# A residual block in fp32r terms on one core: sixteen gate and up chunk pairs of the second feed-forward as 2 by 2 block products with seven products, and all down weight sums made in the first feed-forward

## The chip, the cores and the metric

One core of one Trainium2 chip runs the whole program in one launch. The metric is device time in microseconds (us) of that core. Three runs of the kernel before gave 1135.78, 1136.21 and 1136.25 us; the median is 1136.21.

## The reference

One decoder layer on x of 512 tokens by 1024 features, in fp32. Cut to what matters here:

```
f = swiglu(rms_norm(h, ffn1_pre_g), ffn1_w_gu, ffn1_w_down)
h = h + 0.5 * rms_norm(f, ffn1_post_g)
m = hybrid_mixer(rms_norm(h, mix_pre_g), ...)
h = h + rms_norm(m, mix_post_g)
f = swiglu(rms_norm(h, ffn2_pre_g), ffn2_w_gu, ffn2_w_down)
h = h + 0.5 * rms_norm(f, ffn2_post_g)

def swiglu(x, w_gu, w_down):
    g, u = jnp.split(x @ w_gu, 2, axis=-1)
    return (silu(g) * u) @ w_down
```

`w_gu` is 1024 by 2 x 2816 and `w_down` 2816 by 1024. 2816 is 22 chunks of 128.

## The kernel before

**Terms.** Each fp32 operand is split into a high and a low part in the matmul's fp32r form, and one product is three matmuls into the same PSUM bank (`mm3`, L147-L150): high by high, high by low, low by high. A weight chunk of 128 x 1024 comes from DRAM into a `wraw` buffer (SP issues the load, L109; six buffers). ACT copies it to the high part (L118), and DVE subtracts that from the raw chunk for the low part (L119). `wsplit` does both, two chunks ahead of the one that `wget` hands out (AHEAD), and the load is asked for six chunks ahead (RAHEAD).

**Stages.** f1 is the first feed-forward: `gate_up` and then `strassen_out`, the down projection. The mixer follows (projections, recurrence, attention, two output projections). f2 is the second feed-forward, with the same two functions.

**gate_up** goes through 22 chunk pairs. Pair j is one gate chunk and one up chunk of 128 of the 2816 columns. Each chunk is `feat_chunk` (L245): 8 slices of 128 features, each a product of 128 x 128 weights by 512 tokens, so 24 matmuls into one bank of 128 x 512, and 48 for the pair. `tail` (L313) then makes silu(gate) times up: in f2 a tanh on ACT (L319) and two DVE operations (L323, L324), in f1 one more DVE operation ahead (L321, the row's norm factor). The pairs of the first half (c of h = 0) and of the second (h = 1) are kept apart, for the down projection. In f2 the first two pairs are `first_four` (L254): four banks, and each chunk in two passes of 256 tokens, so that PE can begin when half of the tokens are normalised.

**Down projection.** `strassen_out` takes the down weights as 2 by 2 blocks (two halves of the 2816 features by two halves of the output columns), and the hidden values as 2 by 2 blocks too (feature halves by token halves), with seven products rather than eight. That needs sums of weight blocks and of hidden blocks. `weight_sums` (L270) makes the weight sums during gate_up of the same stage: for each of 11 chunks it loads two raw chunks (L275), makes four adds of 128 x 512 on DVE (L280), and stores the four sums to DRAM (L282), from where the down projection loads them as weights. Its steps are spaced in ticks, one tick for each weight chunk that PE has been given: three ticks for a chunk of sums. `sum_pairs` (L288) makes the sums of hidden blocks for two pairs at a time (L294, L295, L297).

**Order.** The scheduler places instructions on in-order engine queues by the order of the program and by buffers coming free. Buffers around the change: 19 of 8 KB for split weights, sums and operands (`b8`), 6 raw weight buffers, 4 of 4 KB (`t4`), 11 of 2 KB (`t2`), 8 PSUM banks.

## Time and profile before

| | |
|---|---|
| median of three runs | 1136.21 us |
| the profiled execution | 1135.31 us |
| its span, first to last instruction | 1133.2 us |
| PE busy | 1125.1 us of the span, 5318 matmuls |
| DVE busy | 741.1 us |
| ACT busy | 491.9 us |
| moved by DMA | 192.68 MB, mean 170 GB/s |
| granted TensorE clock | 0.999 |
| f1 gate_up | from 4.7 to 295 us |
| f2 gate_up | from 779.8 to 1022 us |

The profile comes from one profiled execution. PE, DVE, ACT, POOL and SP are the engines; PEld is the loading of weights into PE, which overlaps with matmuls. In a row of a list of groups stand the line, the engine, the operation, out<-in by names, the shape and the count, then busy time and mean duration. In a timeline row stand the start and the duration in us, then engine, line and operation; `xN` means N instructions in a run. Square brackets give the idle time ahead of it and what ended that. A matmul's duration covers the pipeline from its start to its last column, so its pace is read from start to start. What lies outside the span is 1135.31 - 1133.2 = 2.1 us.

### The profile page before, as it was taken

The page shows a single profiled execution, that of the slowest core. Times are in us where ns is not written, and L with a number is a line of the kernel's source. Part 1 is how long each engine was busy: PE and PEld are TensorE (multiplying, and loading weights), DVE is VectorE, ACT ScalarE, POOL GpSimd, SP SyncE. Part 2 cuts the span into 40 slices and gives each one's busy share as a digit, 9 for nine tenths or more (in the row PEclk, how much of TensorE's full clock was granted, in tenths as well). Part 3 has the DMA queues.
Part 4 walks back from the last instruction along what each step waited for, and adds up shares of the span by engine and source line. Part 5 has one row for each costly group of instructions (what it writes and reads, how often), then busy time and mean ns, then how long its engine had stood idle before and what let it go on. Part 6 is the DMA issues. An engine that isn't in the chain of part 4 may idle for free.

```text
span 1133.2 us, 14097 instructions
## 1 busy us (share of the span) xinstructions
PE 1125.1 (99%) x5318; PEld 938.0 (83%) x5318; DVE 741.1 (65%) x1122; ACT 491.9 (43%) x767; POOL 25.0 (2%) x47
## 2 busy tenths in 40 slices
PE   9999999999999999999999999999999999999997
PEld 7888888888888887888888888889888888888886
DVE  5674475677787779796776745636553564648784
ACT  6332122255754588453655633414331131236671
POOL 1000000000000000000000000001000000000001
PEclk9999999999999999999999999999999999999999
DMA  9773493546766213334211323533636655616582
GB/s 362 275 288 135 177 333 118 203 152 194 231 248 223 93 64 104 112 98 136 83 57 56 106 81 103 210 134 123 259 129 252 223 206 199 227 60 203 190 281 75
DMA packets 63957, 192.68 MB, mean 170 GB/s; under 512 B 7824, under 2 KB 8592, under 8 KB 61072
## 3 DMA queue, kind: packets, MB, share of 16 engines
q1 hardware_dynamic: 59136, 176.56, 44.2%
q10 hardware_dynamic: 4752, 15.21, 3.8%
q8 instruction: 42, 0.69, 0.2%
q14 instruction: 27, 0.22, 0.1%
HBM read 160.28 MB, written 29.36 MB: 167 GB/s over the span
## 4 chain that ended last, share of the span: by engine, by line
PE 98%; ACT 2%; DVE 0%; issue 0%; POOLq 0%; POOL 0%; DVEq 0%
PE f1g L149 7%; PE f1g L150 7%; PE f1g L148 7%; PE f2g L149 6%; PE f2g L148 6%; PE f2g L150 6%; PE f1x L148 2%; PE f1x L149 2%; PE f2x L148 2%; PE f2x L150 2%; PE f2x L149 2%; PE f1x L150 2%; PE glg L148 1%; PE gag L148 1%; PE gt L150 1%; PE gag L149 1%
## 5 line engine op out<-in xcount | busy, mean ns | idle before, releaser
L119 DVE TENSOR_TENSOR w<-wraw,w 128x1024 fp32r<-128x1024 f32 x238 | 278.7, 1189 | 39.1 <-ACT w L118 38.3
L118 ACT CAST w<-wraw 128x1024 fp32r<-128x1024 f32 x238 | 233.3, 1023 | 105.4 <-PE f1g L150 18.3
L149 PE MATMUL f1g<-u1l,w 128*128 128x512 f32 x336 | 130.8, 389 | 0.0
L148 PE MATMUL f1g<-u1h,w 128*128 128x512 f32 x336 | 130.8, 389 | 0.0
L150 PE MATMUL f1g<-u1h,w 128*128 128x512 f32 x336 | 130.7, 389 | 0.0
L148 PE MATMUL f2g<-b2uh,w 128*128 128x512 f32 x320 | 124.5, 389 | 0.0
L149 PE MATMUL f2g<-b2ul,w 128*128 128x512 f32 x320 | 124.5, 389 | 0.0
L150 PE MATMUL f2g<-b2uh,w 128*128 128x512 f32 x320 | 124.5, 389 | 0.0
L319 ACT ACTIVATE f2s<-f2g 128x512 f32<-128x512 f32 x20 | 12.0, 600 | 145.0 <-PE f2g L150 145.0
L148 PEld LDWEIGHTS f1g<-u1h,w 128*128 128x128 f32 x336 | 63.1, 188 | 13.2
L149 PEld LDWEIGHTS f1g<-u1l,w 128*128 128x128 f32 x336 | 63.1, 188 | 13.2
L150 PEld LDWEIGHTS f1g<-u1h,w 128*128 128x128 f32 x336 | 63.1, 188 | 12.9
L148 PEld LDWEIGHTS f2g<-b2uh,w 128*128 128x128 f32 x320 | 60.1, 188 | 12.5
L150 PEld LDWEIGHTS f2g<-b2uh,w 128*128 128x128 f32 x320 | 60.1, 188 | 12.5
L149 PEld LDWEIGHTS f2g<-b2ul,w 128*128 128x128 f32 x320 | 60.1, 188 | 12.3
L322 ACT ACTIVATE f1s<-f1s 128x512 f32<-128x512 f32 x22 | 13.9, 632 | 128.5 <-DVE f1s L321 128.5
L324 DVE SCALAR_TENSOR_TENSOR f2p<-f2s,f2g 128x512 f32<-128x512 f32 x20 | 13.7, 686 | 58.1 <-PE f2g L150 58.1
L323 DVE SCALAR_TENSOR_TENSOR f2s<-f2s,f2g 128x512 f32<-128x512 f32 x20 | 13.7, 685 | 45.2 <-ACT f2s L319 45.2
L324 DVE SCALAR_TENSOR_TENSOR f1p<-f1s,f1g 128x512 f32<-128x512 f32 x22 | 15.0, 686 | 42.3 <-PE f1g L150 42.1
L321 DVE TENSOR_TENSOR f1s<-f1g,rows 128x512 f32<-128x512 f32 x22 | 15.1, 689 | 32.8 <-PE f1g L150 32.7
L148 PE MATMUL glg<-b1uh,w 128*128 128x512 f32 x64 | 25.8, 403 | 0.0
L148 PE MATMUL glp<-ylh,w 128*128 128x512 f32 x64 | 25.4, 397 | 0.0
(720 smaller groups left out, 2450.4 us busy)
## 6 DMA issues: line engine op xcount, KB each, us to landing
wraw<-in_gu_dram SPq DMA_DIRECT2D x86, 512.0 KB, 5.4
wraw<-t_spill SPq DMA_DIRECT2D x88, 256.0 KB, 3.8
wraw<-in_dn_dram SPq DMA_DIRECT2D x66, 256.0 KB, 5.3
f1tr<-in_dn_dram SPq DMA_DIRECT2D x22, 512.0 KB, 6.4
t_spill<-f1ts SPq DMA_DIRECT2D x11, 1024.0 KB, 7.5
f2tr<-in_dn_dram SPq DMA_DIRECT2D x22, 512.0 KB, 6.4
t_spill<-f2ts SPq DMA_DIRECT2D x11, 1024.0 KB, 7.5
wraw<-in_w_x_dram SPq DMA_DIRECT2D x8, 512.0 KB, 4.5
```

Of the source, the lines that this page charges most:

```text
L118: A.copy(w[:, 0, :end], raws[n][:, :end])
L119: V.tensor_tensor(out=w[:, 1, :end], in0=raws[n][:, :end], in1=w[:, 0, :end].bitcast(F32), op=ALU.subtract)
L148: PE.matmul(o, lhsT=ah, rhs=bh, start=start, stop=False, skip_group_check=more)
L149: PE.matmul(o, lhsT=ah, rhs=bl, start=False, stop=False, skip_group_check=more)
L150: PE.matmul(o, lhsT=al, rhs=bh, start=False, stop=stop, skip_group_check=more)
L319: A.activation(s, bg, AF.Tanh, scale=0.5)
L321: V.tensor_tensor(out=s, in0=bg, in1=rows, op=ALU.mult)
L322: A.activation(s, s, AF.Tanh, scale=0.5)
L323: V.scalar_tensor_tensor(out=s, in0=s, scalar=1.0, in1=bg, op0=ALU.add, op1=ALU.mult)
L324: V.scalar_tensor_tensor(out=ps[h][-1][:, c % 4, :], in0=s, scalar=0.5, in1=bu, op0=ALU.mult, op1=ALU.mult)
```

## The change

**Block products.** Pairs 3 to 18 of f2 (BLOCK_PAIRS) are no longer two chunks of 24 matmuls. The 1024 features are halved, the 512 tokens are halved, and gate and up form the third index: four outputs of 128 x 256, each a sum over two feature halves. The scheme of the down projection gives them with seven products. A product is 4 slices of 128 features, three matmuls each, of 128 x 256: 12 matmuls, 84 for the pair. PE's order within a pair is p1 into bank X, p7 into Y, p6 onto X, p2 into Z, q5 onto X, q4 into Y, q3 onto X (`Blocks.run`). Between them ACT and DVE take partial sums out of the banks: `kv` is p1 in its first half and p7 in its second, `ua` is X after p6 and after q5, `up` and `g` are the up and gate outputs.

**Operands.** The sums of input blocks are made once (`Blocks.operands`, during first_four): two adds of 128 x 2048 on DVE that join high and low again, four sums of 128 x 1024, and four splits of 128 x 1024. Each pair needs four sums of weight blocks of 128 x 512 on DVE (`steps`), and splits of 1024 columns three times and of 512 once (ACT copy, DVE subtract): the gate chunk `g`, the sums `st` 1 and 0, and `d`. The weights of pair j + 1 are made while pair j runs. ACT's and DVE's order in these pairs is written out (`line` chains each instruction behind the one before).

**Weight sums.** Both sets of 11 chunks of down weight sums are made in f1's gate_up, the second set for f2, at 1, 1, 2, 2 ticks a chunk, and none in f2. The next raw chunks are loaded right behind the store.

**Hidden sums.** For the block pairs `sum_pairs` runs once for up to four pairs, behind the last block pair (`later`).

The diff, cut to its core:

```
+BLOCK_PAIRS = range(3, 19)
...
-        while len(wready) < min(upto, len(worder)):
+        while len(wready) < min(upto, len(worder), *stops[:1]):
...
                 if tok is HALVES[1]:
+                    next(extra, None)
                     done(i, bs[i])
...
-    def weight_sums(dn, scr, name, wait):
+    def weight_sums(wait):
         yield wait
-        for c in range(KH):
-            raw = b8(f"{name}tr{c}", [P, 2, 1024])
-            for i in range(2):
-                SP.dma_start(raw[:, i, :], dn[c + i * KH])
-            yield 2
+        todo_ = [(dn, scratch[f], f, c) for f, dn in enumerate((dn1, dn2)) for c in range(KH)]
+        loaded = []
+
+        def load():
+            if len(loaded) < len(todo_):
+                dn, _, f, c = todo_[len(loaded)]
+                raw = b8(f"tr{f}{c}", [P, 2, 1024])
+                for i in range(2):
+                    SP.dma_start(raw[:, i, :], dn[c + i * KH])
+                loaded.append(raw)
+
+        load()
+        yield 2
+        for n, (dn, scr, f, c) in enumerate(todo_):
+            raw = loaded[n]
             b11, b12, b21, b22 = (raw[:, i, hc] for i in range(2) for hc in (slice(0, 512), slice(512, 1024)))
-            ts = b8(f"{name}ts{c}", [P, 4, 512])
+            ts = b8(f"ts{f}{c}", [P, 4, 512])
             for o, a, b in ((0, b11, b12), (1, ts[:, 0], b22), (2, ts[:, 1], b21), (3, b12, b22)):
                 V.tensor_tensor(out=ts[:, o], in0=a, in1=b, op=ALU.add)
-            yield 1
             SP.dma_start(scr[c], ts)
-
-    def gate_up(u, name, dn, scr, rows=None, marks=None):
+            load()
+            yield 1 + n % 4 // 2
...
+        def operands(self, marks):
+            u, name, (A1, A2) = self.u, self.name, self.toks
+            self.ops, self.last["v"] = {}, marks["low", NT - 1]
+            (a, b), xs = self.f, self.xs
+            for i in range(2):
+                self.line("v", V.tensor_tensor, out=self.f[i], in0=u[0][i].bitcast(F32), in1=u[1][i].bitcast(F32),
+                          op=ALU.add)
+            yield
+            wsplit(wpos[0] + AHEAD)
+            yield
+            self.line("v", V.tensor_tensor, out=xs[:, 0], in0=b[:, :, A2], in1=a[:, :, A2], op=ALU.subtract)
+            self.line("v", V.scalar_tensor_tensor, out=xs[:, 1], in0=xs[:, 0], scalar=-1.0, in1=a[:, :, A1],
+                      op0=ALU.mult, op1=ALU.subtract)
+            self.line("v", V.tensor_tensor, out=a[:, :, A2], in0=a[:, :, A1], in1=a[:, :, A2], op=ALU.subtract)
+            self.line("v", V.scalar_tensor_tensor, out=b[:, :, A1], in0=xs[:, 1], scalar=-1.0, in1=b[:, :, A1],
+                      op0=ALU.mult, op1=ALU.subtract)
+            for prod, src in (("p7", a[:, :, A2]), ("p6", xs[:, 1]), ("q5", xs[:, 0]), ("q3", b[:, :, A1])):
+                d = b8(f"{name}x{prod}", [P, 2, 4, T // 2], F32R)
+                A.copy(d[:, 0], src)
+                self.line("v", V.tensor_tensor, out=d[:, 1], in0=src, in1=d[:, 0].bitcast(F32), op=ALU.subtract)
+                self.ops[prod] = d[:, 0], d[:, 1]
...
+        def steps(self, j):
+            n = self.base + 2 * j
+            assert len(wready) == n
+            rg, ru = raws[n:n + 2]
+            fs = [t4(f"{self.name}bf{j}{i}") for i in range(2)]
+            t0, t1, t2_, t3 = (f[:, hc] for f in fs for hc in (slice(0, 512), slice(512, 1024)))
+            b11, b12, b21, b22 = (r[:, hc] for hc in (slice(0, 512), slice(512, 1024)) for r in (rg, ru))
+            for o, x_, y_ in ((t3, b12, b22), (t0, b11, b12), (t1, t0, b22), (t2_, t1, b21)):
+                self.line("v", V.tensor_tensor, out=o, in0=x_, in1=y_, op=ALU.add)
+            g = b8(f"{self.name}bg{j}", [P, 2, 1024], F32R)
+            self.line("a", A.copy, g[:, 0], rg)
+            self.low(g[:, 1], rg, g[:, 0])
+            yield
+            st = [b8(f"{self.name}bs{j}{i}", [P, 2, 1024], F32R) for i in range(2)]
+            self.line("a", A.copy, st[1][:, 0], fs[1])
+            self.low(st[1][:, 1], fs[1], st[1][:, 0])
+            yield
+            self.line("a", A.copy, st[0][:, 0], fs[0])
+            self.low(st[0][:, 1], fs[0], st[0][:, 0])
+            yield
+            d = t4p.tile([P, 2, 512], F32R, name=f"{self.name}bd{j}", tag="t4")
+            self.line("a", A.copy, d[:, 0], b22)
+            self.low(d[:, 1], b22, d[:, 0])
+            wready.extend([None, None])
+            wload(n + 2 + RAHEAD)
+            yield
+            hs_ = [(st[i][:, 0, hc], st[i][:, 1, hc]) for i in range(2) for hc in (slice(0, 512), slice(512, 1024))]
+            self.ready[j] = {"p1": (g[:, 0, :512], g[:, 1, :512]), "p2": (g[:, 0, 512:], g[:, 1, 512:]),
+                             "q3": (d[:, 0], d[:, 1]), "q5": hs_[0], "p6": hs_[1], "q4": hs_[2], "p7": hs_[3]}
...
+        def product(self, o, prod, j, opens):
+            wh, wl = self.ready[j][prod]
+            xh, xl = self.ops[prod]
+            with tc.issue_after(self.last["pe"].ins) if "pe" in self.last else nullcontext():
+                for k in range(4):
+                    ks = slice(k * P, (k + 1) * P)
+                    last = mm3(o, wh[:, ks], wl[:, ks], xh[:, k, :], xl[:, k, :], opens and k == 0, k == 3, not opens)
+            self.last["pe"] = last
...
+        def run(self, j, more):
+            nm = f"{self.name}b"
+            A1, A2 = self.toks
+            X, Y, Z = (bank(f"{nm}{i}{j}")[:, A1] for i in "xyz")
+            kv, ua, g, s, up = (t2(f"{nm}{i}{j}") for i in ("kv", "ua", "g", "s", "up"))
+            steps = self.steps(j + 1) if more else iter([wsplit(wpos[0] + 3), wsplit(wpos[0] + 4)])
+            next(steps, None)
+            self.finish()
+            self.product(X, "p1", j, True)
+            self.line("a", A.copy, kv[:, A1], X)
+            self.product(Y, "p7", j, True)
+            tick()
+            self.line("a", A.copy, kv[:, A2], Y)
+            self.product(X, "p6", j, False)
+            self.line("a", A.copy, ua[:, A1], X)
+            next(steps, None)
+            self.product(Z, "p2", j, True)
+            self.line("v", V.tensor_tensor, out=g[:, A1], in0=Z, in1=kv[:, A1], op=ALU.add)
+            next(steps, None)
+            next(steps, None)
+            self.product(X, "q5", j, False)
+            self.line("a", A.copy, ua[:, A2], X)
+            self.product(Y, "q4", j, False)
+            tick()
+            self.line("v", V.tensor_tensor, out=up[:, A2], in0=ua[:, A2], in1=kv[:, A2], op=ALU.add)
+            self.line("v", V.tensor_tensor, out=g[:, A2], in0=Y, in1=ua[:, A1], op=ALU.add)
+            self.line("a", A.activation, s, g, AF.Tanh, scale=0.5)
+            self.product(X, "q3", j, False)
+            self.line("a", A.copy, up[:, A1], X)
+            for _ in steps:
+                pass
+            self.ended = (j, s, g, up)
...
-            if h and (c % 2 or c == KH - 1):
+            if h and (c % 2 or c == KH - 1) and j not in block_pairs:
...
-            first_four(u, f"{name}f", done, marks)
-        start(weight_sums(dn, scr, name, 6 if rows is not None else 2))
+            stops.append(base + 2 * block_pairs[0])
+            blocks = Blocks(u, name, base, ps)
+            extra = blocks.operands(marks)
+            first_four(u, f"{name}f", done, marks, extra)
+            for _ in extra:
+                pass
+            blocks.prepare(block_pairs[0])
+        else:
+            start(weight_sums(6))
         for j in range(2 if rows is None else 0, KF):
             bb = []
+            if j in block_pairs:
+                last = j == block_pairs[-1]
+                if last:
+                    stops.clear()
+                blocks.run(j, not last)
+                wpos[0] += 2
+                if last:
+                    for q in range(0, block_pairs[-1] - KH + 1, 4):
+                        later.append((q, min(q + 3, block_pairs[-1] - KH)))
+                continue
...
+            while later:
+                sum_pairs(*later.pop(0))```

**In f1's gate_up, DVE, before.** L119 are low parts of weights, L280 down weight sums, L321, L323 and L324 the tail of a pair.

```order
L280 TENSOR_TENSOR f1ts_1129<-f1tr_1060 128x512 x2
L119 TENSOR_TENSOR w_1069<-wraw_858,w_1069 128x1024
L280 TENSOR_TENSOR f1ts_1129<-f1ts_1129,f1tr_1060 128x512
L119 TENSOR_TENSOR w_1099<-wraw_888,w_1099 128x1024
L280 TENSOR_TENSOR f1ts_1129<-f1ts_1129,f1tr_1060 128x512
L321 TENSOR_TENSOR f1s_1134<-f1g_1074,rows_175 128x512
```

The four adds of one chunk of sums stand around two low parts here, and a tail follows.

**The like place after.** L121 are the low parts, L293 the down weight sums, L467 a tail's first operation.

```order
L293 TENSOR_TENSOR ts_951<-tr_882 128x512 x2
L121 TENSOR_TENSOR w_891<-wraw_662,w_891 128x1024
L293 TENSOR_TENSOR ts_951<-ts_951,tr_882 128x512
L121 TENSOR_TENSOR w_921<-wraw_692,w_921 128x1024
L121 TENSOR_TENSOR w_965<-wraw_736,w_965 128x1024
L293 TENSOR_TENSOR ts_995<-tr_957 128x512
L293 TENSOR_TENSOR ts_951<-ts_951,tr_882 128x512
L293 TENSOR_TENSOR ts_995<-tr_957 128x512
L121 TENSOR_TENSOR w_1004<-wraw_775,w_1004 128x1024
L467 TENSOR_TENSOR f1s_960<-f1g_896,rows_175 128x512
```

Before, one chunk of sums lies among two low parts; now two chunks of sums (`ts_951`, `ts_995`) lie interleaved among four.

**In f2's gate_up, DVE, before,** from the tail of one pair to that of the next but one, some pairs into the stage: L119 low parts, L280 weight sums, L323 and L324 tails.

```order
L119 TENSOR_TENSOR w_7158<-wraw_6951,w_7158 128x1024
L324 SCALAR_TENSOR_TENSOR f2p_6908<-f2s_6982,f2g_6953 128x512
L280 TENSOR_TENSOR f2ts_7153<-f2ts_7153,f2tr_7086 128x512
L323 SCALAR_TENSOR_TENSOR f2s_7051<-f2s_7051,f2g_6991 128x512
L280 TENSOR_TENSOR f2ts_7153<-f2ts_7153,f2tr_7086 128x512
L324 SCALAR_TENSOR_TENSOR f2p_6908<-f2s_7051,f2g_7021 128x512
L323 SCALAR_TENSOR_TENSOR f2s_7119<-f2s_7119,f2g_7060 128x512
```

Two tails follow one another here with adds of weight sums between them and no low part.

**After, one whole block pair on DVE,** but for the last row of its thirteen. Every row has the line of the helper (L334). `f2bf` are sums of weight blocks, `f2bg` ahead of a `wraw` the low part of the next gate chunk, `f2bs` ahead of `f2bf` the low parts of the sums (7086 is st 1, 7085 is st 0), `f2bd` the low part of d; the two SCALAR_TENSOR_TENSOR are the tail of the pair before; the 256-wide rows read PSUM banks.

```order
L334 TENSOR_TENSOR f2bf_7036<-wraw_6753 128x512
L334 TENSOR_TENSOR f2bf_7035<-wraw_6748,wraw_6753 128x512
L334 TENSOR_TENSOR f2bf_7035<-f2bf_7035,wraw_6753 128x512
L334 TENSOR_TENSOR f2bf_7036<-f2bf_7035,wraw_6748 128x512
L334 TENSOR_TENSOR f2bg_7041<-wraw_6748,f2bg_7041 128x1024
L334 SCALAR_TENSOR_TENSOR f2bs_6910<-f2bs_6910,f2bg_6909 128x512
L334 SCALAR_TENSOR_TENSOR f2p_6755<-f2bs_6910,f2bup_6911 128x512
L334 TENSOR_TENSOR f2bs_7086<-f2bf_7036,f2bs_7086 128x1024
L334 TENSOR_TENSOR f2bg_7032<-f2bz_7029,f2bkv_7030 128x256
L334 TENSOR_TENSOR f2bs_7085<-f2bf_7035,f2bs_7085 128x1024
L334 TENSOR_TENSOR f2bd_7104<-wraw_6753,f2bd_7104 128x512
L334 TENSOR_TENSOR f2bup_7034<-f2bua_7031,f2bkv_7030 128x256
```

The thirteenth row is `f2bg_7032<-f2by_7028,f2bua_7031`, 128x256, the gate's second half. Before, low parts of weights ran far ahead of PE in groups and only the tails were tied to a pair; now every instruction of DVE is tied to its pair.

**ACT in the same block pair, after.** `f2bkv`, `f2bua` and `f2bup` are copies out of the banks X and Y, the wide CASTs are the high parts of the next pair's weights, ACTIVATE is the tanh.

```order
L334 CAST f2bg_7041<-wraw_6748 128x1024
L334 COPY f2bkv_7030<-f2bx_7027 128x256
L334 COPY f2bkv_7030<-f2by_7028 128x256
L334 COPY f2bua_7031<-f2bx_7027 128x256
L334 CAST f2bs_7086<-f2bf_7036 128x1024
L334 CAST f2bs_7085<-f2bf_7035 128x1024
L334 CAST f2bd_7104<-wraw_6753 128x512
L334 COPY f2bua_7031<-f2bx_7027 128x256
L334 ACTIVATE f2bs_7033<-f2bg_7032 128x512
L334 COPY f2bup_7034<-f2bx_7027 128x256
```

Before, ACT had two wide casts and one tanh for a pair in this stage, and PE waited for its casts only; now four copies of partial sums stand between the casts, and PE's products onto X wait for them.

**DVE where the first block pair (pair 3) takes over from pair 2, after.** L470 is the last operation of pair 2's tail, which reads pair 2's up bank (`f2g_6875`); `f2bs_6838` is st 1 of pair 3.

```order
L334 TENSOR_TENSOR f2bf_6829<-f2bf_6828,wraw_6307 128x512
L334 TENSOR_TENSOR f2bg_6834<-wraw_6307,f2bg_6834 128x1024
L470 SCALAR_TENSOR_TENSOR f2p_6755<-f2s_6900,f2g_6875 128x512
L334 TENSOR_TENSOR f2bs_6838<-f2bf_6829,f2bs_6838 128x1024
L334 TENSOR_TENSOR f2bs_6837<-f2bf_6828,f2bs_6837 128x1024
```

Here the low parts st 1 and st 0 of pair 3 stand behind an operation that can only start when PE has ended pair 2; before, no low part of the next pair stood behind that operation.

More of the change, by code (lines that the diff above doesn't have):

```diff
@@ L102, in hybrid_block_kernel @@
     trail = []
+    stops = []
     def wload(upto):
@@ L149, in mm3 @@
         PE.matmul(o, lhsT=ah, rhs=bl, start=False, stop=False, skip_group_check=more)
-        PE.matmul(o, lhsT=al, rhs=bh, start=False, stop=stop, skip_group_check=more)
+        return PE.matmul(o, lhsT=al, rhs=bh, start=False, stop=stop, skip_group_check=more)
     def gain_pair(i, n, name):
@@ L252, in hybrid_block_kernel, with first_four @@
     HALVES = (slice(0, T // 2), slice(T // 2, T))
-    def first_four(u, name, done, marks):
+    def first_four(u, name, done, marks, extra):
         ws, bs = [wget(0), wget(0)], [bank(f"{name}{i}") for i in range(4)]
@@ L285, in gate_up @@
+    def gate_up(u, name, rows=None, marks=None):
         ps, sums = [[], []], []
@@ L289, in sum_pairs @@
             q = lo // 4
-            if lo % 4 == 0:
+            if len(sums) == q:
                 sums.append(b8(f"{name}sum{q}", [P, 4, 2, T // 2]))
@@ L324, in tail @@
             V.scalar_tensor_tensor(out=ps[h][-1][:, c % 4, :], in0=s, scalar=0.5, in1=bu, op0=ALU.mult, op1=ALU.mult)
-            if h and (c % 2 or c == KH - 1):
+            if h and (c % 2 or c == KH - 1) and j not in block_pairs:
                 sum_pairs(c - c % 2, c)
-        bs, late = [], []
+        bs, late, later = [], [], []
+        block_pairs = BLOCK_PAIRS if rows is None else ()
+        base = wpos[0]
         def done(i, b):
@@ L352, in gate_up @@
             late.append((j, bb))
+            while later:
+                sum_pairs(*later.pop(0))
             if rows is None or j > 0:
@@ L569, in hybrid_block_kernel @@
     start(row_scale())
-    down1 = gate_up(u1, "f1", dn1, scratch[0], rows1)
+    down1 = gate_up(u1, "f1", rows1)
     u2 = []
@@ L916, in hybrid_block_kernel @@
     token_out(lambda c: mg[c // 4], KD, epilogue, "wo", TAILS[1])
-    down2 = gate_up(u3, "f2", dn2, scratch[1], marks=epilogue.marks)
+    down2 = gate_up(u3, "f2", marks=epilogue.marks)
     strassen_out(down2, Boundary(hs2, ov, lambda: gain_pair(5, 1, "g_b3"), None, 0.5, "b3"), "f2", TAILS[2])
```

33 lines of the change are left out of this document (added).

## The prediction

> **What bounds the kernel now.** I read the page's busy shares, the chain that ended last and PE's waits first.
>
> ```profile
> PE 1125.1 (99%) x5318; PEld 938.0 (83%) x5318; DVE 741.1 (65%) x1122; ACT 491.9 (43%) x767; POOL 25.0 (2%) x47
> PE 98%; ACT 2%; DVE 0%; issue 0%; POOLq 0%; POOL 0%; DVEq 0%
> PE warm L181 <- POOL ident masks.py:199: 1.4, 1, 1.4
> PE r L148 <- ACT xch L632: 0.6, 1, 0.6
> ```
>
> PE is busy for 1125.1 of 1133.2 us, it makes 98% of the chain, and its waits come to 2.0 us in all. So only two things can change the time: how long PE's own stream is, and new waits in it. DVE at 65% and ACT at 43% have room on average, so the second question is where they have none.
>
> Next I read the pace of PE from start to start. The f2 gate and up matmuls of 512 columns, as the tile's rows show them:
>
> ```profile
> L148 PE MATMUL f2g<-b2uh,w x320: 389/389/396, 804.6 to 1021.6; 128*128 128x512 f32 x160
> L150 PE MATMUL f2g<-b2uh,w x320: 389/389/389, 805.1 to 1022.0; 128*128 128x512 f32 x160
> ```
>
> There are 3 x 320 = 960 of them, the first at 804.6 and the last at 1022.0, so 217.4 / 959 = 0.2267 us from one to the next. The same stage also holds a stretch of 256 columns, in first_four:
>
> ```profile
> 781.06 0.28 PE L149 MATMUL f2f<-b2ul,w 128*128 128x256 f32 x1
> 781.17 0.28 PE L150 MATMUL f2f<-b2uh,w 128*128 128x256 f32 x1
> 781.29 0.28 PE L148 MATMUL f2f<-b2uh,w 128*128 128x256 f32 x1
> ...
> 789.21 0.28 PE L150 MATMUL f2f<-b2uh,w 128*128 128x256 f32 x1
> ```
>
> The timeline has 67 matmul rows in this stretch, and in two places a gap of just two steps where a record is missing, so 69 matmuls and 68 steps: (789.21 - 781.06) / 68 = 0.120 us. Chunks end every 24 matmuls, so at least two changes of weights and bank lie in this stretch, and none shows a gap.
>
> **The change, PE's part.** A pair before is 48 x 0.2267 = 10.88 us. A block pair is 84 x 0.120 = 10.08 us. PE saves 0.80 us a pair, over 16 pairs 12.8 us. The order of PE's instructions has 16 x 36 = 576 more matmuls, as 84 - 48 demands. A step shorter by 0.001 us would save 84 x 16 x 0.001 = 1.3 us more.
>
> [...]
>
> **The change, DVE and ACT in a block pair.** Their durations, from the groups by line with shapes apart:
>
> ```profile
> L119 DVE TENSOR_TENSOR w<-wraw,w 128x1024 fp32r<-128x1024 f32 x224 | 269.4, 1220 | 37.8 <-ACT w L118 37.1 <-DMA wraw<-t_spill 0.2
> L280 DVE TENSOR_TENSOR f2ts<-f2tr 128x512 f32<-128x512 f32 x22 | 14.7, 685 | 0.0
> L712 DVE TENSOR_TENSOR kp<-kt,kp 128x256 fp32r<-128x256 f32 x4 | 1.6, 420 | 0.6 <-ACT kp L711 0.6
> L118 ACT CAST w<-wraw 128x1024 fp32r<-128x1024 f32 x224 | 225.8, 1049 | 105.4 <-PE f1g L150 18.3 <-issue 14.1 <-PE glp L150 10.8
> L118 ACT CAST w<-wraw 128x512 fp32r<-128x512 f32 x14 | 8.6, 617 | 0.0
> L711 ACT CAST kp<-kt 128x256 fp32r<-128x256 f32 x4 | 1.4, 370 | 3.0 <-PE kt L722 3.0
> ```
>
> In a run an instruction starts before the one ahead has ended. The timeline around 800 us and in f1 shows by how much:
>
> ```profile
> 796.53 0.60 ACT L319 ACTIVATE f2s<-f2f 128x512 f32<-128x512 f32 x1 [5.48 <-PE f2f L150]
> 797.02 5.78 ACT L118 CAST w<-wraw 128x1024 fp32r<-128x1024 f32 x6
> 797.16 0.69 DVE L323 SCALAR_TENSOR_TENSOR f2s<-f2s,f2f 128x512 f32<-128x512 f32 x1 [5.28 <-ACT f2s L319]
> 799.89 2.35 DVE L119 TENSOR_TENSOR w<-wraw,w 128x1024 fp32r<-128x1024 f32 x2
> 802.16 0.68 DVE L280 TENSOR_TENSOR f2ts<-f2tr 128x512 f32<-128x512 f32 x1
> 802.70 0.60 ACT L319 ACTIVATE f2s<-f2f 128x512 f32<-128x512 f32 x1
> ...
> 148.10 0.69 DVE L294 TENSOR_TENSOR f1sum<-f1p,f1p 128x512 f32<-128x512 f32 x1
> 148.82 0.69 DVE L295 SCALAR_TENSOR_TENSOR f1sum<-f1sum,f1p 128x512 f32<-128x512 f32 x1
> 149.43 0.69 DVE L297 TENSOR_TENSOR f1p<-f1p 128x512 f32<-128x512 f32 x1
> ```
>
> DVE, start to start: (802.16 - 799.89) / 2 = 1.135 for 1024 columns; 0.60 for 512 (148.82 to 149.43), 0.72 where it reads the result just ahead (148.10 to 148.82). For 256 I estimate 0.335, the 0.42 of L712 less the same 0.085. ACT: (802.70 - 797.02) / 6 = 0.95 for 1024, 0.49 for 512 (796.53 to 797.02), and 0.28 for 256, estimated likewise from L711. From ACT's end to DVE's start is 0.03 (796.53 + 0.60 to 797.16).
>
> DVE's thirteen rows of a block pair: sums 0.60 + 0.72 + 0.72 + 0.60, low parts 3 x 1.135 + 0.60, tail 2 x 0.60 (0.72 and 0.60 if chained), three of 256 columns 3 x 0.335: 8.97 us with the chained steps as printed above, 9.7 by full durations. ACT: 3 x 0.95 + 0.49 + 0.50 + 5 x 0.28 = 5.2. PE has 10.08. So neither is the bound by its load.
>
> The order written out makes a ring through three engines, and this is the place to watch. From PE's start of p6 of pair j: last matmul of the product 1.32 later, its end +0.28, hop 0.04; ACT copies `ua` (0.28) and makes st 1 high (1.05); hop 0.03; DVE low of st 1 (1.135), first half of g (0.335), low of st 0 (1.135), low of d (0.60), up (0.335), second half of g (0.42); hop 0.03; ACT tanh (0.50), up (0.28), high of the next g (0.95), first half of the next `kv` (0.37); hop 0.05; p6 of pair j + 1 may start. The sum is 9.14 us, and with every duration in full 9.95. Both are under 10.08, so PE stays the bound and the ring costs nothing, but with a margin of only 0.9 to 0.1 us. I take nothing for it, because DVE's and ACT's runs in the rows quoted do overlap; the other end, a ring of 10.3 (9.95, hops twice as long, 0.15, and a load of weights that waits with p6, 0.19), costs 16 x 0.22 = 3.5 us.
>
> **The hand-over from pair 2 to pair 3.** DVE's rows there, before:
>
> ```profile
> 790.59 1.29 DVE L213 TENSOR_TENSOR b2ul<-b2ntp,b2uh 128x512 fp32r<-128x512 f32 x2 [2.29 <-ACT b2uh L212]
> ...
> 811.98 0.68 DVE L324 SCALAR_TENSOR_TENSOR f2p<-f2s,f2f 128x512 f32<-128x512 f32 x1
> 812.58 0.68 DVE L323 SCALAR_TENSOR_TENSOR f2s<-f2s,f2g 128x512 f32<-128x512 f32 x1
> 815.71 0.69 DVE L324 SCALAR_TENSOR_TENSOR f2p<-f2s,f2g 128x512 f32<-128x512 f32 x1 [2.45 <-PE f2g L150]
> ```
>
> Pair 2's last operation on DVE starts at 815.71, when its up bank is ready; PE itself goes on at 804.6 + 48 x 0.2267 = 815.5. The low part of st 1 stands behind that operation: start 815.71 + 0.60, end 1.22 later, 817.53. p1 of pair 3 covers 815.5 to 816.95, and the first low matmul of p7, its third, would start at 817.2. PE stalls about 0.35 us, once. Ahead of it DVE has the operands' work, from 791.9, where the last low part of the input ends: two adds of 2048 columns (estimated at twice 1.135), eight operations and three low parts of weights at 1024 (11 x 1.135), five of the tails and four sums of 512 (5.6), 22.6 us, so to 814.5. The gate chunk's low part is the last of these, and p1 wants it at 815.7. So this too is nearly full. I take 0.35, with 0 and 2 as ends.
>
> **The weight sums, moved.** Taken out of f2: 44 adds, 22 loads, 11 stores; nothing there waits for them (no L280 among PE's releasers), so this brings PE nothing, but it frees DVE for the blocks. Put into f1:
>
> ```profile
> 28.00:292.00 264.00, 264.00 (x1166) 218.58 (x1165) 170.07 (x225) 87.42 (x103) 0.00 (x0) 1.00 0.58 206
> 806.00:1013.00 207.00, 207.00 (x915) 171.47 (x914) 100.96 (x131) 47.29 (x56) 0.00 (x0) 1.00 0.55 202
> f1tr<-in_dn_dram SPq DMA_DIRECT2D x22, 512.0 KB, 6.4
> t_spill<-f1ts SPq DMA_DIRECT2D x11, 1024.0 KB, 7.5
> 76.00:88.00 12.00, 12.00 (x54) 9.95 (x53) 5.47 (x9) 0.63 (x1) 0.00 (x0) 1.00 1.02 415
> ```
>
> Columns of the windows: length, then busy PE, PEld, DVE, ACT, POOL, then the clock, the DMA share and GB/s. In f1, DVE is busy 170.07 of 264 us; 44 adds x 0.685 add 30, so 200. Within the time of dense sums a pair has 4/3 chunks of sums (3.5 us), two low parts (2.3) and a tail (1.8), 7.6 of 10.88 us. DMA moves 206 GB/s at a share of 0.58, and up to 415 in a burst; the 23 MB more (11 x 2 loads of 512 KB and a store of 1 MB) need 56 us at that speed, and 0.42 x 264 = 111 us are free. Weights are asked for six chunks, 33 us, ahead, and the longest pile in front of one in SP's queue is two stores and four loads, 4 MB, 10 us. I walked through DVE's new order row by row with these prices: each chunk's low part is done at least 4.5 us before PE wants it. So I take nothing; the other end, a few chunks late by a store's 7.5 us less that 4.5, is up to 6 us for two of them.
>
> **The sum.** Of the profiled execution: 1135.31 - 12.8 + 0.35 = 1122.9. The median of the runs lies 0.9 above that execution: 1123.8.
>
> **The rivals.**
>
> *The ring is longer than 10.08 us.* For it: the margin is 0.1 us by full durations. Against it: the runs overlap in every row quoted. At 10.3 it is 1123.8 + 3.5 = 1127.3; only above 10.88 does it eat the whole gain. Chance 0.15.
>
> *f1 starves.* For it: DVE at 7.6 of 10.88 with an in-order queue where tails wait for PE, and buffers of `b8` held by stores of 7.5 us. Against: the leads above. 1 to 6 us, so 1125 to 1130; chance 0.10.
>
> *Weight loads are not pulled ahead over a product's wait.* This ends slower. In first_four the loads fill PEld:
>
> ```profile
> 782.00:788.00 6.00, 6.00 (x52) 6.00 (x51) 5.27 (x7) 1.15 (x2) 0.55 (x1) 1.00 0.49 175
> L148 PEld LDWEIGHTS f2f<-b2uh,w x64: 188/192/192, 779.6 to 804.1; 128*128 128x128 f32 x64
> ```
>
> PEld is busy 6.00 of 6.00 us there, and one load takes 0.192 against a step of 0.120, so loads have to overlap. Each of seven products starts with a wait of its own. If every one costs a load that nothing hides, a pair is 10.08 + 7 x 0.192 = 11.42, 0.54 longer than before: 16 x 0.54 + 0.35 gives 1136.2 + 9.0 = 1145.2. It decides from 0.80 / 7 = 0.115 us a product. Against it: chunk changes in the 256-column stretch show no gap. Chance 0.06. [...]
>
> *PE is faster still.* The step in the block pairs is 0.118 or less, since no transposes stand among them: 12.8 + 2.7 saved, 1121 or under. Chance 0.03. [...]
>
> The change does what it says: the matmul count of the order shows it.
>
> **How the numbers follow.** The forecast, PE-bound block pairs and a quiet f1, has 0.66. Low end 1122.0: no stall at the hand-over, 1123.4, and a step shorter by 0.001 us, 84 x 16 x 0.001 = 1.3. High end 1131.0: 1123.8 with the ring at 10.3 (3.5), f1 late by half of its 6 us (3) and a third of the hand-over's other end (0.6). Beyond it lie the weight loads and the worst of ring and f1, about 0.10 together; below the low end lies 0.03. A measurement of this kernel can tell about 0.2%, 2.3 us, from no change. Faster: the forecast 0.66, 0.13 of the ring, 0.08 of f1, 0.03: 0.90. Same 0.03: a ring near 10.8, or f1 late in many places. Slower 0.07: the weight loads and the rest of ring and f1.
>
> **What would show it.** In the profile after, matmuls of a block pair should follow at 0.120, and 16 pairs should take 161 us rather than 174, with p1 to p1 at 10.08. DVE should sit idle about 1 us in each pair ahead of st 1's low part, released by ACT. One stall of some 0.35 us should stand at p7 of pair 3, released by DVE. In f1's window PE should still be busy 264.00 of 264, with DVE near 200 and a DMA share near 0.8. I am wrong if PE's waits list a few tenths at p6 or q5 sixteen times (the ring), if a wait on L121 or on a load shows in f1, or if steps at the start of products are longer than within them (the loads).

## The result and the profile after

| | before | after |
|---|---|---|
| median of runs | 1136.21 us (5 runs, 1135.76 to 1136.39) | 1124.07 us (5 runs, 1123.29 to 1124.64) |
| the profiled execution, its span | 1135.31, 1133.2 us | 1124.64, 1122.5 us |

The ratio is 0.9894, 95% interval 0.9879 to 0.9908: 12.1 us faster. The forecast was 1123.8.

The page's busy shares of the kernel after, its chain, and PE's waits:

```profile
PE 1113.6 (99%) x5894; PEld 955.4 (85%) x5894; DVE 838.7 (75%) x1270; ACT 546.5 (49%) x883; POOL 25.0 (2%) x47
PE 97%; ACT 2%; DMA 0%; DVE 0%; issue 0%; SPq 0%; POOLq 0%; DVEq 0%
PE warm L183 <- POOL ident masks.py:199: 1.4, 1, 1.4
PE r L150 <- ACT xch L799: 0.6, 1, 0.6
PE f1g L710 <- ACT u1h L700: 0.6, 1, 0.6
PE f2by L152 <- DVE f2bs L334: 0.2, 1, 0.2
```

PE is still the chain. It has 5894 matmuls, 576 more, and is busy 11.5 us less. Two waits are new: one in the opening (f1g, line 710) and one at the hand-over (f2by), which was forecast. The list names no wait at p6 or q5 and none at a weight of f1. Waits too short for the list show in the timeline as longer steps: 0.27 instead of 0.12 at q3 of pair 3, with 0.23 behind it, and one of 0.22 to 0.23 each at p6 of pair 4 and q3 of pair 17. In the pairs between, no step is longer than 0.13 us, at the starts of products neither.

Block pairs, by the first matmul of each (p1 of pairs 5, 6 and 17 in PE's timeline), and the hand-over at p7 of pair 3:

```profile
837.81 0.28 PE L150 MATMUL f2bx<-b2uh,f2bg 128*128 128x256 f32 x1
847.89 0.28 PE L150 MATMUL f2bx<-b2uh,f2bg 128*128 128x256 f32 x1
...
958.59 0.28 PE L150 MATMUL f2bx<-b2uh,f2bg 128*128 128x256 f32 x1
...
818.38 0.28 PE L151 MATMUL f2by<-f2xp,f2bs 128*128 128x256 f32 x1
818.90 0.39 PE L152 MATMUL f2by<-f2xp,f2bs 128*128 128x256 f32 x1 [0.25 <-DVE f2bs L334]
819.12 0.28 PE L150 MATMUL f2by<-f2xp,f2bs 128*128 128x256 f32 x1
```

(958.59 - 837.81) / 12 = 10.065 us a pair, where 10.08 was forecast. At the hand-over the step is 0.52 instead of 0.12: 0.40 lost, 0.35 forecast. The matmul that waited also takes 0.39, and the next comes 0.22 later instead of 0.12. So PE lost 0.1 us here beyond the wait itself (a restart, in what follows), which I had not reckoned with.

DVE and ACT in one steady block pair (DVE's rows, then ACT's; the pair runs from p1 at 878.07 to 888.15):

```profile
880.47 1.22 DVE L334 TENSOR_TENSOR f2bg<-wraw,f2bg 128x1024 fp32r<-128x1024 f32 x1
881.61 0.68 DVE L334 SCALAR_TENSOR_TENSOR f2bs<-f2bs,f2bg 128x512 f32<-128x512 f32 x1
882.33 0.69 DVE L334 SCALAR_TENSOR_TENSOR f2p<-f2bs,f2bup 128x512 f32<-128x512 f32 x1
884.00 1.23 DVE L334 TENSOR_TENSOR f2bs<-f2bf,f2bs 128x1024 fp32r<-128x1024 f32 x1 [0.98 <-ACT f2bs L334]
885.14 0.42 DVE L334 TENSOR_TENSOR f2bg<-f2bz,f2bkv 128x256 f32<-128x256 f32 x1
885.48 1.21 DVE L334 TENSOR_TENSOR f2bs<-f2bf,f2bs 128x1024 fp32r<-128x1024 f32 x1
```

```profile
881.15 0.37 ACT L334 COPY f2bkv<-f2by 128x256 f32<-128x256 f32 x1 [1.04 <-PE f2by L152]
882.65 0.37 ACT L334 COPY f2bua<-f2bx 128x256 f32<-128x256 f32 x1 [1.12 <-PE f2bx L152]
882.92 2.00 ACT L334 CAST f2bs<-f2bf 128x1024 fp32r<-128x1024 f32 x2
```

DVE sits idle for 0.98 us ahead of st 1's low part, released by ACT, as forecast (about 1 us). The steps are those of the prediction: 1.14 for 1024 columns, 0.34 for 256 (an estimate then), 0.72 for a chained 512. ACT's rows show that it waits 1.04 and 1.12 us for PE, so it has room too.

The windows of f1's gate_up and of f2's:

```profile
28.00:292.00 264.00, 264.00 (x1169) 218.56 (x1168) 194.37 (x268) 86.40 (x101) 0.00 (x0) 1.00 0.79 294
806.00:1013.00 207.00, 206.75 (x1544) 198.43 (x1543) 178.69 (x245) 110.33 (x183) 0.00 (x0) 1.00 0.32 103
```

In f1, DVE has 194 of 264 us (200 forecast) and DMA a share of 0.79 (0.8 forecast); PE is busy throughout.

**Where the time went.** The down projection's first matmul is at 1022.2 before and 1011.6 after, 10.6 us earlier; from there on both kernels take the same. But f1's first chunk behind the opening starts 1.3 us later in this execution (16.14 before, 17.47 after), so f2's gate_up gained 11.9. Sixteen pairs x (10.88 - 10.065) = 13.0; the first two block pairs take 0.85 us more than the steady ones (10.83 and 10.16), the last two some 0.1 to 0.2. The later opening is hardly the change's: the same opening starts that chunk between 16.0 and 17.1 us in the profiles of the experiments, at 16.3 where only the weight sums are moved (sums_only), and at 16.9 in one built on the kernel before.

### The profile page after: what moved, and what is told of

Read it like the earlier page. It is cut to its first block, busy times and chain, and to the rows that moved or that the text cites. A ratio compares the mean times of both kernels' runs of the same rounds, so it can differ in the third digit from the quotient of the medians.

```text
span 1122.5 us, 15503 instructions
## 1 busy us (share of the span) xinstructions
PE 1113.6 (99%) x5894; PEld 955.4 (85%) x5894; DVE 838.7 (75%) x1270; ACT 546.5 (49%) x883; POOL 25.0 (2%) x47
## 4 chain that ended last, share of the span: by engine, by line
PE 97%; ACT 2%; DMA 0%; DVE 0%; issue 0%; SPq 0%; POOLq 0%; DVEq 0%
PE f1g L150 7%; PE f1g L151 7%; PE f1g L152 7%; PE f2bx L150 3%; PE f2bx L152 3%; PE f2bx L151 3%; PE f1x L150 2%; PE f1x L152 2%; PE f2x L151 2%; PE f2x L152 2%; PE f2x L150 2%; PE f1x L151 2%; PE glg L150 1%; PE f2by L152 1%; PE f2by L151 1%; PE f2by L150 1%
## 5 line engine op out<-in xcount | busy, mean ns | idle before, releaser
L121 DVE TENSOR_TENSOR w<-wraw,w 128x1024 fp32r<-128x1024 f32 x206 | 239.9, 1184 | 37.0 <-ACT w L120 33.7
L120 ACT CAST w<-wraw 128x1024 fp32r<-128x1024 f32 x206 | 202.3, 1020 | 106.2 <-DVE ts L293 16.2
L150 PE MATMUL f1g<-u1h,w 128*128 128x512 f32 x336 | 130.8, 389 | 0.0
L151 PE MATMUL f1g<-u1l,w 128*128 128x512 f32 x336 | 130.8, 389 | 0.0
L152 PE MATMUL f1g<-u1h,w 128*128 128x512 f32 x336 | 130.7, 389 | 0.0
L152 PEld LDWEIGHTS f1g<-u1h,w 128*128 128x128 f32 x336 | 63.1, 188 | 13.2
L150 PEld LDWEIGHTS f1g<-u1h,w 128*128 128x128 f32 x336 | 63.1, 188 | 13.1
L151 PEld LDWEIGHTS f1g<-u1l,w 128*128 128x128 f32 x336 | 63.1, 188 | 13.0
L334 DVE TENSOR_TENSOR f2bs<-f2bf,f2bs 128x1024 fp32r<-128x1024 f32 x32 | 39.0, 1221 | 13.0 <-ACT f2bs L334 13.0
L470 DVE SCALAR_TENSOR_TENSOR f1p<-f1s,f1g 128x512 f32<-128x512 f32 x22 | 15.0, 684 | 29.2 <-PE f1g L152 29.1
L334 ACT CAST f2bs<-f2bf 128x1024 fp32r<-128x1024 f32 x32 | 32.0, 1050 | 3.7 <-DVE f2bf L334 3.7
L467 DVE TENSOR_TENSOR f1s<-f1g,rows 128x512 f32<-128x512 f32 x22 | 15.0, 687 | 21.3 <-PE f1g L152 21.1
L293 DVE TENSOR_TENSOR ts<-tr 128x512 f32<-128x512 f32 x44 | 29.5, 684 | 1.1 <-DMA tr<-in_dn_dram 1.1
L293 DVE TENSOR_TENSOR ts<-ts,tr 128x512 f32<-128x512 f32 x44 | 29.8, 683 | 0.3 <-DMA tr<-in_dn_dram 0.3
L334 ACT ACTIVATE f2bs<-f2bg 128x512 f32<-128x512 f32 x16 | 10.1, 634 | 32.7 <-DVE f2bg L334 32.7
L150 PE MATMUL glg<-b1uh,w 128*128 128x512 f32 x64 | 25.8, 403 | 0.0
L150 PE MATMUL glp<-ylh,w 128*128 128x512 f32 x64 | 25.4, 397 | 0.0
L150 PE MATMUL gag<-b1uh,w 128*128 128x512 f32 x64 | 25.4, 396 | 0.0
L150 PE MATMUL q<-b1uh,w 128*128 128x512 f32 x64 | 25.1, 393 | 0.0
L150 PE MATMUL x<-b1uh,w 128*128 128x512 f32 x64 | 25.1, 392 | 0.0
L151 PE MATMUL gag<-b1ul,w 128*128 128x512 f32 x64 | 25.0, 391 | 0.0
```

The costliest lines, as they stand in the source:

```text
L120: A.copy(w[:, 0, :end], raws[n][:, :end])
L121: V.tensor_tensor(out=w[:, 1, :end], in0=raws[n][:, :end], in1=w[:, 0, :end].bitcast(F32), op=ALU.subtract)
L150: PE.matmul(o, lhsT=ah, rhs=bh, start=start, stop=False, skip_group_check=more)
L151: PE.matmul(o, lhsT=ah, rhs=bl, start=False, stop=False, skip_group_check=more)
L152: return PE.matmul(o, lhsT=al, rhs=bh, start=False, stop=stop, skip_group_check=more)
L293: V.tensor_tensor(out=ts[:, o], in0=a, in1=b, op=ALU.add)
```

## The experiments

My theory: PE's step of 0.120 us at 256 columns sets a pair, a ring through ACT and DVE with some 0.8 us of slack and DVE's load with some 0.9 us stay under it, and f1 had room for the sums. The rivals were a ring or a load that binds, f1 starved, and loads of weights exposed. The runs come from three chips, on which the kernel before took 1135.69, 1135.89 and 1135.62 us; each ratio is to the kernel before on the same chip.

**The weight sums alone** (sums_only).

```
-BLOCK_PAIRS = range(3, 19)
+BLOCK_PAIRS = ()
```

with first_four called without the operands. 

> The weight sums of both down projections are made in f1, and no pair is a block product. My theory: f1 has room (DVE 194 of 264 us and a DMA share of 0.79 in the window from 28 to 292 us, PE busy throughout), and in f2 nothing waited for the sums, so the time is that of before, 1136.2, within 0.5 us. Rival: the moved sums cost something in f1 or at its start that the gain of the block pairs hides: 1 to 2 us slower, 1137 to 1138, with PE idle in f1.

Measured: 1136.06 us, ratio 1.0002 (0.9994 to 1.0011). Its windows:

```profile
28.00:292.00 264.00, 264.00 (x1166) 218.56 (x1166) 195.47 (x269) 87.67 (x103) 0.00 (x0) 1.00 0.79 293
806.00:1013.00 207.00, 207.00 (x915) 171.41 (x914) 75.04 (x88) 46.79 (x56) 0.00 (x0) 1.00 0.27 96
```

PE is full in both, though DVE does 25 us more in f1 and 26 us less in f2. The move by itself is worth nothing, in either stage, within 0.1%: the gain comes with the block pairs.

**The block pairs alone** (blocks_only). `weight_sums` as in the kernel before, started in each stage:

```
-        else:
-            start(weight_sums(6))
+        start(weight_sums(dn, scr, name, 6 if rows is not None else 2))
```

> Sixteen block pairs, and each stage makes its own weight sums as before. My theory: DVE has 0.92 us idle in a block pair of 10.07, so 9.15 of work; two thirds of a chunk of sums a pair (2.64 us a chunk) add 1.76, and 10.9 is over PE's 10.07. 11 chunks are 29 us, of which 16 x 0.92 = 15 fit into the idle time: 14 us lost, about 1137, and PE waits in nearly every block pair for DVE's low parts or partial sums. Rival: the sums slip into the idle time or behind the block pairs, as off-path work: 1124 to 1127.

Measured: 1133.90 us, ratio 0.9983 (0.9974 to 0.9992): ten of the twelve us are lost again. PE's waits, and f2's window:

```profile
PE f2bx L150 <- ACT f2bkv L323: 5.5, 7, 1.5
PE f2bx L150 <- ACT f2bua L323: 1.6, 2, 1.1
...
806.00:1013.00 207.00, 199.33 (x1499) 190.33 (x1498) 192.47 (x279) 103.12 (x175) 0.00 (x0) 1.00 0.58 203
```

From p1 to p1 it is 10.0 to 11.8 us, 10.7 on average; PE waits at p6 for the first half of `kv` (on the ring), or at q3 for `ua`. So the move, worth nothing alone, is what makes the block pairs pay. DVE has next to no room left: it is busy for 166.3 of the 171 us from 815 to 986, and its own waits there are for ACT and PE, not for a load. The loss, 10.2 us (f2's gate_up takes 240.7 us in the profile instead of 230.4), is smaller than the 14 I expected: by my reckoning 40 adds, not 44, fall into the 160 us of block pairs (26.6 us), and DVE's own work there is 9.0 rather than 9.15 us a pair, as sum3 shows below, so 16 x 1.07 us of them fit; that leaves 9.5.

**More on the ring** (tanh4), a fourfold tanh.

```
-            self.line("a", A.activation, s, g, AF.Tanh, scale=0.5)
+            for _ in range(4):
+                self.line("a", A.activation, s, g, AF.Tanh, scale=0.5)
```

> The changed kernel with the tanh of each block pair done four times over, into the same tile: 3 x 0.50 = 1.5 us more of ACT a pair, on the ring. My theory: the ring has 0.8 us of slack in the profile after (the first half of kv ends 0.79 before p6 starts), so a pair grows by 0.7 us: 16 x 0.7 = 11 us, 1135, with PE waiting at p6 onto X. Rival: only loads count; ACT then has 6.7 of 10.07 us and nothing changes, 1124.

Measured: 1144.76 us, ratio 1.0076 (1.0062 to 1.0090), 21 us over the changed kernel, with pairs of 11.23. One whole turn of the ring, from p6 to p6 (PE's, ACT's and DVE's rows):

```profile
888.41 0.38 PE L150 MATMUL f2bx<-f2xp,f2bs 128*128 128x256 f32 x1 [0.92 <-ACT f2bkv L334]
...
890.14 0.37 ACT L334 COPY f2bua<-f2bx 128x256 f32<-128x256 f32 x1 [1.51 <-PE f2bx L152]
890.41 2.00 ACT L334 CAST f2bs<-f2bf 128x1024 fp32r<-128x1024 f32 x2
...
891.49 1.22 DVE L334 TENSOR_TENSOR f2bs<-f2bf,f2bs 128x1024 fp32r<-128x1024 f32 x1 [0.82 <-ACT f2bs L334]
892.63 0.42 DVE L334 TENSOR_TENSOR f2bg<-f2bz,f2bkv 128x256 f32<-128x256 f32 x1
...
895.04 0.42 DVE L334 TENSOR_TENSOR f2bg<-f2by,f2bua 128x256 f32<-128x256 f32 x1
...
895.49 2.63 ACT L334 ACTIVATE f2bs<-f2bg 128x512 f32<-128x512 f32 x4 [2.09 <-DVE f2bg L334]
898.02 0.35 ACT L334 COPY f2bup<-f2bx 128x256 f32<-128x256 f32 x1
898.27 1.05 ACT L334 CAST f2bg<-wraw 128x1024 fp32r<-128x1024 f32 x1
899.22 0.37 ACT L334 COPY f2bkv<-f2bx 128x256 f32<-128x256 f32 x1
...
899.65 0.39 PE L150 MATMUL f2bx<-f2xp,f2bs 128*128 128x256 f32 x1 [0.91 <-ACT f2bkv L334]
```

The ring is there, link by link as the prediction listed it, and binds: 899.65 - 888.41 = 11.24 us. The four tanh take 898.02 - 895.49 = 2.53, one takes 0.54 in the kernel after (888.06 to 888.60), so the ring with one is 9.25, of which 0.1 is PE's restart: 9.15, where the prediction had 9.14. My expectation of the time, 1135, was 10 us too low, for three reasons that the rows show. Four activations onto the same tile follow at 0.66 us from start to start and not at 0.50, and PE's restart comes on top in every pair. And pair 4 takes 13.6 us, and pair 18 is drawn out likewise: the waits there are longer, 1.83 and 2.20 us, and the granted clock fell behind them. The window behind the first:

```profile
831.70:835.20 3.50, 3.50 (x19) 3.50 (x19) 1.83 (x4) 1.36 (x3) 0.00 (x0) 0.52 0.50 149
```

For 3.5 us the clock stands at 0.52 and the step is 0.21 instead of 0.12, which costs about 1.5 us at each of the two places (17 steps take 3.53 us instead of 2.04 in pair 4). So some 3 of the 21 us are the clock and not the ring.

PE's weight loads at the same p6 show what goes with a restart:

```profile
888.41 0.19 PEld L150 LDWEIGHTS f2bx<-f2xp,f2bs 128*128 128x128 f32 x1 [1.13 <-ACT f2bkv L334]
888.52 0.19 PEld L151 LDWEIGHTS f2bx<-f2xp,f2bs 128*128 128x128 f32 x1
...
888.64 0.28 PE L151 MATMUL f2bx<-f2xp,f2bs 128*128 128x256 f32 x1
```

The second load starts 0.12 us ahead of its matmul (888.52 and 888.64), much as one in a steady pair of the kernel after does (837.70, its matmul 837.81). Behind the wait the load starts with its matmul, both at 888.41, as at all 16 waits of 0.2 us or more in the block pairs of this run: at none of them was it pulled ahead over the wait. This is the prediction's rival of exposed loads, true where PE does wait, at 0.1 us and not 0.192, and without effect in the changed kernel, whose steady pairs have no wait.

**The like load off the ring** (kv6).

```
-            self.line("a", A.copy, kv[:, A2], Y)
+            for _ in range(6):
+                self.line("a", A.copy, kv[:, A2], Y)
```

> The changed kernel with the second half of kv copied six times over: 5 x 0.28 = 1.4 us more of ACT a pair, nearly the load of the tanh experiment, but where ACT waits about 1.1 us for p6 to end. My theory: at most 0.3 us of it reaches the ring, which has 0.8 us of slack, so 1124 within 0.7 us. Rival, that ACT's load in a pair counts wherever it lies: as slow as the tanh experiment, 1135.

Measured: 1126.09 us, ratio 0.9912 (0.9897 to 0.9927). ACT's load grew by 2.0 us a pair (six copies from 880.45 to 882.75, where one takes 0.27), as much as with the tanh (2.53 less 0.54), for a tenth of the price: load as such doesn't count. But 2.4 us is more than I allowed. PE's rows show why, at q5:

```profile
883.01 0.28 PE L152 MATMUL f2bz<-b2uh,f2bg 128*128 128x256 f32 x1
883.18 0.39 PE L150 MATMUL f2bx<-f2xq,f2bs 128*128 128x256 f32 x1
883.40 0.28 PE L151 MATMUL f2bx<-f2xq,f2bs 128*128 128x256 f32 x1
```

`ua` came 0.05 us too late for q5 and PE lost 0.15, in every pair from 5 on (10.21 instead of 10.065). That edge has a slack of its own, which the copies used up, and the 0.05 of waiting cost three times its length there. Pair 17 alone takes 10.98 instead of 10.19: PE waits 0.5 us at q3 for `ua`, whose copy stands behind a high part of an ordinary weight chunk there. That is about a third of the 2.4 us.

**More of DVE, in its idle time** (sum3).

```
-            for o, x_, y_ in ((t3, b12, b22), (t0, b11, b12), ...
+            for o, x_, y_ in ((t3, b12, b22), (t3, b12, b22), (t3, b12, b22), (t0, b11, b12), ...
```

> The changed kernel with the first sum of weight blocks of each block pair made three times: 2 x 0.60 = 1.2 us more of DVE a pair, at the place where DVE then sits idle (0.92 us ahead of st 1's low part). My theory: DVE's work in a pair becomes 9.15 + 1.2 = 10.35, over PE's 10.07, so DVE's load is the bound: 16 x 0.28 = 4.5 us, with a restart of 0.1 us a wait 6 at most, 1128 to 1130, and DVE's idle time ahead of st 1 is gone. Rival, that only the ring counts, and that these sums lie off it: 1124.

Measured: 1132.11 us, ratio 0.9968 (0.9956 to 0.9979). DVE's rows:

```profile
882.25 2.14 DVE L334 TENSOR_TENSOR f2bf<-wraw 128x512 f32<-128x512 f32 x3
884.30 0.69 DVE L334 TENSOR_TENSOR f2bf<-wraw,wraw 128x512 f32<-128x512 f32 x1
...
888.82 1.22 DVE L334 TENSOR_TENSOR f2bs<-f2bf,f2bs 128x1024 fp32r<-128x1024 f32 x1
...
892.70 0.68 DVE L334 TENSOR_TENSOR f2bf<-wraw 128x512 f32<-128x512 f32 x1
```

DVE's idle time ahead of st 1's low part is gone, and from one first sum to the next it is 892.70 - 882.25 = 10.45 us, the period of the pairs (10.44): DVE's load binds. The three adds take 2.05 us where one takes 0.60, so DVE's work without the two is 10.45 - 1.45 = 9.0 us; the prediction had 8.97. The time lies above the 1128 to 1130 that I expected. The rest of the loss, 3.2 us, is at the start, where pair 3 takes 14.07 us instead of 10.83: PE waits 2.3 us in it for the low part of the gate chunk, and 1.2 us at q3. DVE's rows ahead of it:

```profile
815.56 0.69 DVE L470 SCALAR_TENSOR_TENSOR f2p<-f2s,f2g 128x512 f32<-128x512 f32 x1 [1.47 <-PE f2g L152]
816.16 0.68 DVE L334 TENSOR_TENSOR f2bf<-f2bf,wraw 128x512 f32<-128x512 f32 x1
816.76 1.22 DVE L334 TENSOR_TENSOR f2bg<-wraw,f2bg 128x1024 fp32r<-128x1024 f32 x1
```

DVE does not lack room there, it sits idle for 1.47 us. With two sums more, pair 2's last operation (L470) came to stand ahead of the last sum and of the gate chunk's low part, and all of them wait for PE to end pair 2. It is the hand-over's wait again, made longer by the order.

**The step at 256 columns by itself** (halves), on the kernel before.

```
-                feat_chunk(b, w, u, ALL)
+                for tok in (ALL,) if rows is not None else HALVES:
+                    feat_chunk(b, w, u, tok)
```

> The kernel before, with the 20 pairs of f2 behind first_four computed in two passes of 256 tokens: 96 matmuls of 256 columns a pair instead of 48 of 512, all else as before. This prices the step by itself. My theory: 96 x 0.120 - 48 x 0.2267 = 0.64 us a pair, 20 pairs 12.8 us more, 1149. [...] Rival, that loads of weights are exposed where a chunk begins: two or more tenths at each pass, over 1165.

Measured: 1148.49 us, ratio 1.0112 (1.0097 to 1.0127): 12.6 us more for 20 pairs, where 0.120 against 0.2267 gives 12.8, as expected.

```profile
L148 PE MATMUL f2g<-b2uh,w x640: 283/283/283, 805.4 to 1035.4; 128*128 128x256 f32 x160
L150 PE MATMUL f2g<-b2uh,w x640: 283/283/283, 805.6 to 1035.7; 128*128 128x256 f32 x160
```

1920 matmuls from 805.4 to 1035.7, 230.3 / 1919 = 0.1200 us. All steps are 0.12 us, so no load is exposed between the 80 passes.

**Two pairs more** (to20).

```
-BLOCK_PAIRS = range(3, 19)
+BLOCK_PAIRS = range(3, 21)
```

> The changed kernel with two block pairs more, 3 to 20. My theory: two pairs more at 10.07 instead of 10.88 save 1.6 us, about 1122.5, as long as the hidden sums fit. Rival: only pair 21 is then left to cover the late hidden sums (nine operations on DVE, some 9 us) ahead of the down projection, which waits: 1124 to 1130, with a wait of PE at the down projection's first products.

Measured: 1121.68 us, ratio 0.9875 (0.9858 to 0.9891). Pairs 17 and 18 now run at 10.08 and 10.06 us, pair 19 at 10.14, pair 20's products lie among those of pair 21, and no wait of PE is listed behind them. The gain over the changed kernel, some 2.2 us against the 1.6 expected, is within the intervals, which overlap.

**The hand-over** (handover).

```
-            V.scalar_tensor_tensor(out=ps[h][-1][:, c % 4, :], ...
+            with tc.issue_after(blocks.last["v"].ins) if rows is None and j == 2 else nullcontext():
+                V.scalar_tensor_tensor(out=ps[h][-1][:, c % 4, :], ...
```

> The changed kernel with pair 2's last operation on DVE put behind the low parts of pair 3 (st 1, st 0, d). Those inputs are ready at 815.9 in the profile after, and DVE waits until 817.0 for pair 2's up bank. My theory: the stall of PE at p7 of pair 3 (0.40 us) and the restart goes, and part of the smaller ones up to p6 of pair 4, 0.5 to 0.85 us in all: pair 3 takes 10.1 to 10.3 us rather than 10.83, and the time is at 1123.3, which the timing can hardly tell from 1124. Rival: DVE then runs late for pair 4 instead, and the stall moves to p6 of pair 4 or to pair 5: pairs 3 and 4 together take 21.0 as after.

Measured: 1122.65 us, ratio 0.9885 (0.9870 to 0.9900). DVE's rows at the place:

```profile
813.91 1.22 DVE L334 TENSOR_TENSOR f2bg<-wraw,f2bg 128x1024 fp32r<-128x1024 f32 x1
815.11 2.36 DVE L334 TENSOR_TENSOR f2bs<-f2bf,f2bs 128x1024 fp32r<-128x1024 f32 x2
817.39 0.68 DVE L334 TENSOR_TENSOR f2bd<-wraw,f2bd 128x512 fp32r<-128x512 f32 x1
817.99 0.68 DVE L471 SCALAR_TENSOR_TENSOR f2p<-f2s,f2g 128x512 f32<-128x512 f32 x1
```

The low parts follow at once, PE's wait at f2by is gone, and pairs 3 and 4 take 10.07 and 10.06 us: 0.86 us less together. So the later excesses of pairs 3 and 4 were the wake of the same wait. That the time fell by this lies within the intervals; the profile shows it.

**Both together** (best), beside the changed kernel once more on the same chip. 

> The changed kernel once more, to stand on the same chip beside the next: 1123.5 to 1124.5, and the first chunk of f1 behind first_pair should start at 16.0 to 16.9 us, as in most of the profiles, and not at 17.5 as in the profile after.

> Both edits that gained: pair 2's last operation behind the low parts of pair 3, and block pairs 3 to 20. My theory: the two add, 0.85 and 1.6 us, so 2.4 us under the changed kernel beside it, about 1121, every block pair at 10.06 us. Rival: with pair 2's tail later, the hidden sums or a buffer come late at the other end, and the two together give no more than one of them, 1121.7 or more, with a wait of PE behind the last block pair.

Measured: 1123.74 us (ratio 0.9893, 0.9877 to 0.9910) and 1121.04 us (ratio 0.9871, 0.9856 to 0.9886): 2.7 us less, against 2.4 expected. The runs of the two don't overlap (1123.38 to 1124.29 and 1120.77 to 1121.34), and the eighteen pairs run from 815.78 to 986.98 at p1, 171.2 / 17 = 10.07 us. My guess on the opening did not hold: the changed kernel's first chunk started at 17.1, that of the other at 16.4.

## Why the prediction was right

- **PE's part** (12.8 us): right. 0.120 us a step held in the block pairs (10.065 / 84 = 0.1198 us) and in halves. At 512 columns the step before was 0.2267, so the ratio of the two is 0.529, under the 48/84 = 0.571 at which a block pair would have saved nothing.
- **The load of DVE and ACT in a pair**: right. 9.0 against 8.97 us of DVE, by sum3. ACT's load counted only where it made a copy late that PE waits for, by kv6 against tanh4.
- **The ring** (9.14 to 9.95, so a margin of 0.9 to 0.1): right, at 9.14. The starts overlapped as in the rows of before; tanh4 gives 9.15 by subtraction. What the prediction lacked is that each of PE's edges has its own slack: q5's, behind `ua`, is used up by 2.0 us of ACT that leave p6's alone.
- **The hand-over** (0.35): the mechanism was right, and the size was off: 0.40 at p7 and, with the restart and the wake in pairs 3 and 4, 0.85 in all. The two ends given, 0 and 2, hold it.
- **The weight sums in f1** (nothing): right, by sums_only. The margins were not tight: transfers grew slower (t_spill 10.0 us to landing instead of 7.5, the raw chunks 9.0 instead of 6.4) without any wait of PE.
- **The sum**: 1123.8 against 1124.07 (and 1123.74 in the repeat). Two small errors partly cancel: the block pairs gave 0.2 us more than reckoned and the hand-over cost 0.5 more. That the sum comes within 0.3 us is in part luck. It starts from one execution before, 0.9 under its median, while the profiled execution after, 1124.64, lies 0.57 above its median and 1.7 above the 1122.9 reckoned for it; its opening, 1.3 us later, accounts for most of that. The prediction had no term for the opening.
- **The rivals**: the ring did not bind and f1 did not starve. Exposed loads would have shown as longer steps at each product; there are none. A small edit brings about the ring (tanh4); sums_only rules out that f1 starves; halves rules out loads exposed where chunks change, and the steady pairs after rule them out at the starts of products. The step didn't fall to 0.118 either, and the reason given for that was empty: the stretch that gave 0.120 holds no transposes itself.

## What to carry to other kernels

Fewer columns a matmul can pay with PE as the bound, when its step at the smaller width is taken from a stretch of the same kernel; here 84 short steps took 7.5% less than 48 long ones (10.065 against 10.88 us). Before counting the gain, add up the other engines' work in one period and follow the ring that their fixed order makes, with times from start to start: durations would have put it within 0.1 us of the bound, start to start 0.9 under it, as measured. And moving work that hides anyway is worth nothing by itself, but can be the condition of the gain: the sums cost nothing in either stage before, and ten of twelve us where the new pairs need DVE. Look at the seams too: the one stall of the change, and most of the surprise in sum3, come from an operation of the old pairs that stands in front of work for the new ones.
